# A gMLP and dilated-attention trunk on one core: combined weights made one stage earlier, the last two half-size products run tile by tile, saved key/value weights kept for every other unit

## The chip, the cores and the metric

The kernel runs on one core of a Trainium2 chip. A core has five engines with instruction queues of their own: TensorE (PE, matrix products; its weight loads are listed apart as PEld), VectorE (DVE), ScalarE (ACT), GpSimd (POOL) and SyncE (SP), which in this kernel issues the DMA transfers, one after the other in the order of its queue. The metric is the device time of the whole kernel in microseconds (us); lower is better. Matmul inputs are rounded to the format fp32r, so each fp32 matrix is kept as a pair hi + lo, and a product is made of three matmuls.

## The reference

Two layers over a sequence of 2048 tokens of width 1024, all fp32. The first is a gated MLP whose tokens are mixed within chunks of 128; the second is sliding-window attention in three dilation groups that read one shared K/V.

```python
def gmlp_layer(x, c, ada_w, ada_b, norm_g, w_in, sgu_g, w_s, b_s, w_out):
    shift, scale, gate = ada_mod(c, ada_w, ada_b, 3)
    h = rms_norm(x, norm_g) * (1 + scale) + shift
    u, v, z = jnp.split(h @ w_in, 3, axis=-1)              # each 2048 wide
    u = jax.nn.gelu(u)
    v = rms_norm(jax.nn.gelu(v), sgu_g)
    mixed = jnp.einsum('gts,bcsge->bctge', jnp.tril(w_s), v chunked) + b_s
    y = u * mixed * jax.nn.silu(z)
    return x + gate * (y @ w_out)                          # 2048 -> 1024

# shared_kv: k, v = split(norm(x) @ w_kv): 6 KV heads of 128, K normalised
# dilated_layer: q, z = norm(x) @ w_in: 24 query heads of 128 in 3 groups
#   (window, dilation) = (128, 1), (512, 4), (2048, 16); a banded softmax per head;
#   groups joined by the softmax of their log-sum-exp; x + gate * ((o * silu(z)) @ w_out)
```

## The kernel before

The sequence is cut into four quarters Q = 0..3 of 512 tokens. Each quarter passes through `layer_A` and then `proj_B`; each stage is a run of products over 512 tokens.

`layer_A` has four stages: v (`dense`, PSUM tiles pd_v), u and z (`dense_f`, pd_u and pd_z, eight blocks j each), and the output product y @ w_out (pd_o), called the out stage here. Quarter 0 makes the output product plainly (`dense`, tiles pd_o0). Quarters 1 to 3 make it with seven half-size products (`dense_s`, a Strassen-Winograd scheme, tiles pd_oQa and pd_oQb), each of eight steps k; a step is 2 token tiles x 3 matmuls on one weight unit. Four of the seven use combinations t1..t4 of the quadrants of w_out. `combine_out` makes these once: it loads the quadrants in 8 slabs, combines them with four POOL subtractions a slab (L349-L352) and stores the results to HBM, those of even k already split into hi and lo (arrays wqs), those of odd k unsplit (wq). The y operands are combined and split by `OutOperands` (`put`).

`proj_B` follows with three key/value blocks `kv_block` n = 2, 1, 0 and the query products between them, in the order kv 2, kv 1, q 2, kv 0, q 1, q 0, z. Blocks 2 and 1 are split in an early quarter and their eight split units are saved to HBM (arrays wk, 512 KB a unit); later quarters load these instead of splitting again (`kv_units`).

A weight unit is 128 x 512 of a weight. `raw_unit` loads it (256 KB, tiles raw_*), ACT writes hi (L246) and DVE, or POOL for some, writes lo (L250) into a tile w_* of a pool of eight buffers; `split_unit` loads a saved split unit (512 KB) and needs neither. All loads and stores stand in SP's single queue in program order as a scheduler settled it, and an issue that waits holds up those behind it.

**Fillers.** The attention of quarter Q-1 has no stage of its own. The generator `attend_local` is put on a list and `tick(part)`, called after every step of a product, advances it by `rate[0]` x part pieces. It runs during v, u and z of quarter Q; what is left is drained. A unit of attention is: transposes of Q and K on PE, scores ps (L1100-L1102), DVE bias and row maxima (L1105, L1108, L1109, L1112), ACT exponential (L1115), POOL on the diagonal block (L1123, L1124, L1126), transposes pp of the probabilities (L1143, L1157) and products po (L1176). POOL L1225 and DVE L1180 join the groups' outputs. `weave` advances `attend_local` and `combine_out` together, one piece of each per call: this is how `combine_out` runs during quarter 1.

Behind the out stage, `scale_out` stores the new residual (x1d, L818) and scales it (xr, L821); `transposed(1)` and `transposed(0)` turn its token tiles with PE transposes pt_b (L566), whose copies hkh and hkl (L572) are the left operand of pd_kv. `transposed(1)` (tiles 2 and 3) is called within the last of the seven products, `transposed(0)` (tiles 0 and 1) is handed on as `tail` and called within the first kv block.

## Time and profile before

| what | us |
|---|---|
| median of 3 runs (3076.18, 3084.06, 3090.19) | 3084.06 |
| the profiled execution's own time | 3080.11 |
| its span, first to last instruction | 3078.4 |
| PE busy | 2951.7 (96%) |
| DVE, ACT, POOL busy | 2100.3, 1658.5, 1014.2 |
| quarter 0: v 27.7-143.1, u to 252.9, z to 340.0, out to 429.0, kv/q/z to 659.7 | |
| quarter 1: v 659.7-766.9, u to 896.7, z to 1013.4, out to 1096.4, kv/q/z to 1341.3 | |
| quarter 2: v 1341.3-1453.0, u to 1576.0, z to 1693.7, out to 1776.2, kv/q/z to 2008.6 | |
| quarter 3: v 2008.6-2119.9, u to 2243.0, z to 2360.4, out to 2444.9, kv/q/z to 2795.5, end 3078.4 | |

Times within a profile count from the first instruction. A line of waits gives the engine that waits and for which tile and line, "<-" the instruction waited for, and then the total, the number and the longest of the waits. A line of windows gives, for each engine, the busy time and the number of instructions, in the order PE, PEld, DVE, ACT, POOL, and then the granted PE clock (1.00 is full), the mean busy share of the DMA engines and GB/s. A line of the timeline has the start, the duration and the instruction, and in brackets how long the engine idled ahead of it and for what.

### The profile page before, as it was taken

How to read it: one execution, taken by the hardware profiler on the slowest of the kernel's cores; microseconds unless marked ns; L12 is line 12 of the kernel's file. 1: busy time of each engine (PE TensorE's matmuls, PEld its weight loads, DVE VectorE, ACT ScalarE, POOL GpSimd, SP SyncE). 2: the span in 40 equal slices, each digit the busy share in tenths (PEclk: the TensorE clock that was granted, in tenths of full speed). 3: DMA queues.
4: the chain of work that ended last, by engine and by line, in shares of the span. 5: the costliest groups of instructions: out<-in, count | busy, mean ns of one | idle time of the engine just before them, and what ended most of it. 6: DMA issues, size and time to landing. Idle time of an engine off the chain costs nothing.

```text
span 3078.4 us, 45400 instructions
## 1 busy us (share of the span) xinstructions
PE 2951.7 (96%) x14784; PEld 2466.3 (80%) x14784; DVE 2100.3 (68%) x3576; ACT 1658.5 (54%) x3368; POOL 1014.2 (33%) x1232
## 2 busy tenths in 40 slices
PE   6999999999999999999999999999999999988999
PEld 5788878787788767788888878788887788867787
DVE  6788466774567777765677776856678677767762
ACT  4333345666456545566366455566466358857540
POOL 4147013344314323423134323423236031133332
PEclk9999999999999999999999999999999999999999
DMA  7899456677733687663433776743334776678742
GB/s 234 265 322 344 154 202 210 216 236 245 246 103 114 224 276 246 210 212 114 134 100 113 250 245 210 249 156 124 108 116 138 257 230 216 224 231 282 247 147 96
DMA packets 363073, 619.14 MB, mean 201 GB/s; under 512 B 38250, under 2 KB 137804, under 8 KB 362836
## 3 DMA queue, kind: packets, MB, share of 16 engines
q1 hardware_dynamic: 362836, 616.24, 61.1%
q8 instruction: 117, 1.92, 0.3%
q14 instruction: 120, 0.98, 0.1%
HBM read 489.61 MB, written 126.49 MB: 200 GB/s over the span
## 4 chain that ended last, share of the span: by engine, by line
PE 48%; DMA 7%; DVE 6%; issue 5%; POOL 3%; ACT 3%; SPq 1%; POOLq 0%; DVEq 0%; ACTq 0%
PE pd_v L293 5%; PE po L1176 3%; PE pd_kv L293 3%; PE pd_u L330 3%; PE pd_u L332 3%; PE pd_u L331 2%; PE pd_z L332 2%; PE pd_z L330 2%; PE pd_z L331 2%; DMA qt<-qd 2%; PE pm L756 1%; PE pf L1353 1%; PE pf L1354 1%; PE pf L1352 1%; PE pd_o2b L293 1%
## 5 line engine op out<-in xcount | busy, mean ns | idle before, releaser
L293 PE MATMUL pd_v<-w_v,hAh 128*128 128x512 f32 x1024 | 329.7, 403 | 3.5 <-ACT hAh L544 1.2
L293 PE MATMUL pd_kv<-w_kv,hkh 128*128 128x512 f32 x768 | 238.1, 392 | 9.2 <-DMA w_kv<-wk 3.8
L293 PEld LDWEIGHTS pd_v<-w_v,hAh 128*128 128x128 f32 x1024 | 190.1, 192 | 44.5 <-DVE w_v L250 2.8
L1115 ACT ACTIVATE pr<-pr,stat,rt 128x256 f32<-128x256 f32 (+1 forms) x320 | 177.6, 556 | 66.0 <-DVE stat L1109 40.1
L332 PE MATMUL pd_u<-hAh,w_u 128*128 128x512 f32 x512 | 202.5, 395 | 7.0 <-DVE w_u L250 7.0
L330 PE MATMUL pd_u<-hAh,w_u 128*128 128x512 f32 x512 | 208.3, 407 | 0.0
L330 PE MATMUL pd_z<-hAh,w_z 128*128 128x512 f32 x512 | 206.4, 403 | 0.0
L293 PE MATMUL pd_v<-w_v,hAl 128*128 128x512 f32 x512 | 203.3, 397 | 0.0
L332 PE MATMUL pd_z<-hAh,w_z 128*128 128x512 f32 x512 | 201.9, 394 | 0.0
L331 PE MATMUL pd_z<-hAl,w_z 128*128 128x512 f32 x512 | 201.1, 393 | 0.0
L331 PE MATMUL pd_u<-hAl,w_u 128*128 128x512 f32 x512 | 201.0, 393 | 0.0
L293 PEld LDWEIGHTS pd_kv<-w_kv,hkh 128*128 128x128 f32 x768 | 142.8, 188 | 43.0 <-ACT hkh L572 4.9
L1123 POOL TENSOR_TENSOR dg<-pr,ident 128x256 f32<-128x256 f32 x76 | 59.9, 788 | 343.8 <-ACT pr L1115 317.7
L246 ACT ACTIVATE w_u<-raw_u 128x512 fp32r<-128x512 f32 x128 | 78.4, 630 | 167.6 <-PE pd_u L332 89.0
L1176 PEld LDWEIGHTS po<-kv,pT 128*128 128x128 f32 x1200 | 147.8, 192 | 10.4 <-ACT pT L1026 3.7
L1176 PE MATMUL po<-kv,pT 128*128 128x128 f32 x1200 | 151.2, 276 | 2.0 <-ACT pT L1026 1.9
L246 ACT ACTIVATE w_z<-raw_z 128x512 fp32r<-128x512 f32 x128 | 78.0, 625 | 138.8 <-PE pd_z L332 58.6
L293 PE MATMUL pd_kv<-w_kv,hkl 128*128 128x512 f32 x384 | 148.5, 390 | 0.0
L250 DVE TENSOR_TENSOR w_u<-raw_u,w_u 128x512 fp32r<-128x512 f32 x128 | 101.2, 804 | 68.4 <-ACT w_u L246 66.8
L959 POOL TENSOR_SCALAR s_q<-s_q 128x4 f32<-128x4 f32 x96 | 23.3, 243 | 366.5 <-DVE s_q L958 338.6
L1105 DVE SCALAR_TENSOR_TENSOR pr<-dist,rt,ps 128x256 f32<-128x256 f32 (+1 forms) x320 | 122.5, 430 | 24.2 <-PE ps L1102 19.1
L250 DVE TENSOR_TENSOR w_z<-raw_z,w_z 128x512 fp32r<-128x512 f32 x128 | 117.6, 937 | 30.4 <-ACT w_z L246 27.9
(748 smaller groups left out, 8248.3 us busy)
## 6 DMA issues: line engine op xcount, KB each, us to landing
raw_q<-in_b_w_in_dram SPq DMA_DIRECT2D x144, 256.0 KB, 4.1
raw_v<-in_a_w_in_dram SPq DMA_DIRECT2D x128, 256.0 KB, 4.4
raw_u<-in_a_w_in_dram SPq DMA_DIRECT2D x128, 256.0 KB, 3.7
raw_z<-in_a_w_in_dram SPq DMA_DIRECT2D x128, 256.0 KB, 2.8
raw_o<-in_a_w_out_dram SPq DMA_DIRECT2D x104, 256.0 KB, 3.0
qt<-qd SPq DMA_DIRECT2D x96, 260.0 KB, 3.3
od<-ot SPq DMA_DIRECT2D x96, 256.0 KB, 2.9
w_kv<-wk SPq DMA_DIRECT2D x40, 512.0 KB, 5.1
```

Of the source, the lines that this page charges most:

```text
L246: nc.scalar.activation(hi, src, AF.Copy)
L250: e.tensor_tensor(lo, src, hi.bitcast(F32), ALU.subtract)
L293: last_mm[0] = nc.tensor.matmul(pt, a, u[:, w, :], start=f, stop=e, skip_group_check=more)
L330: nc.tensor.matmul(pts[i], wh, hh[:, k, :], start=k == 0, stop=False)
L331: nc.tensor.matmul(pts[i], wh, hl[:, k, :], start=False, stop=False)
L332: nc.tensor.matmul(pts[i], wl, hh[:, k, :], start=False, stop=k == KT - 1)
L756: nc.tensor.matmul(pm[:, t * P:(t + 1) * P], m[e // 8][:, t, (e % 8) * P:(e % 8 + 1) * P], wst[:, e // 2, :], start=True, stop=True)
L1105: nc.vector.scalar_tensor_tensor(pr[:, i, :], dist[:, 256 - w:256], u["rt"][:, h:h + 1], psc[:, i, :], ALU.mult, ALU.add)
L1115: nc.scalar.activation(pr[:, i, :], pr[:, i, :], AF.Exp, bias=mneg[:, i:i + 1], scale=u["rt"][:, h:h + 1], accum_out=lsum[:, i:i + 1])
L1123: nc.gpsimd.tensor_tensor(dg, prev, ident.unsqueeze(1).broadcast_to([P, hp, P]), ALU.mult)
L1176: nc.tensor.matmul(po[:, h * P:(h + 1) * P], u["pT"][h // hp][:, h % hp, j, :], u["kv"][:, j, kh, 1, :], start=j == 0, stop=j == nk - 1)
L1352: nc.tensor.matmul(pt, yb[:, 0, k, :], wh[:, k, :], start=k == 0, stop=False)
```

## The change

1. `combine_out` no longer runs beside the attention in quarter 1. It is put on the filler list at the start of quarter 0's out stage, with a rate of 1.6 where the rate was 0. It stages its slabs in tiles of the attention (qt, qT, pr, pT) instead of xin, as four loads of 256 KB a slab, and runs as a pipeline in which slab k is loaded while slab k-1 is stored. Only t2 and t3 at even k are stored split; t1 and t4, and odd k, are stored raw, and for raw units of t1 and t4 with k % 3 == 1 POOL makes the lo part.
2. The attention's rate goes from 1.4 to 1.5.
3. In quarters 1 to 3 the last two of the seven products run all 24 matmuls of token tile 0, then its additions and output, and then those of tile 1. `transposed(1)` comes after k = 2 of tile 1 of the last product.
4. Of the saved kv blocks only the even units are saved and loaded split; the odd ones are loaded raw and split each time.
5. `transposed(0)` is called at k = 6 of the first kv block instead of k = 4.
6. In `OutOperands`, half of the lo parts of operand "12" go from DVE to POOL.

```diff
 def kv_units(Q, n, nm):
-        if n == 0 or Q < 2 - n:
-            return wunits(w_kv, 0, n * 512, nm)
-        if Q > 2 - n:
-            return [split_unit(rows_of(wk2[n], k), f"{nm}{k}") for k in range(KT)]
-        us = wunits(w_kv, 0, n * 512, nm)
-        for k, u in enumerate(us):
-            nc.sync.dma_start(rows_of(wk2[n], k), u.bitcast(F32))
+        saved = n and Q > 2 - n
+        us = []
+        for k in range(KT):
+            if saved and k % 2 == 0:
+                us.append(split_unit(rows_of(wk2[n], k // 2), f"{nm}{k}"))
+                continue
+            us.append(raw_unit(w_kv[k * P:(k + 1) * P, n * 512:(n + 1) * 512], f"{nm}{k}"))
+            if n and Q == 2 - n and k % 2 == 0:
+                nc.sync.dma_start(rows_of(wk2[n], k // 2), us[k].bitcast(F32))
         return us
...
-                    if mid and pr == prs[0] and k == KT // 2:
+                    if mid and pr == prs[0] and k == KT - 2:
                         mid()
...
         def load(k):
-            hold[k] = [xp.tile([P, 2, 512], F32, tag="xin", name=f"co{k}{r}") for r in range(2)]
-            for r in range(2):
-                nc.sync.dma_start(hold[k][r], ...)
+            if k % 2:
+                t = [ap_.tile([P, 520], F32, tag="qt", name=f"co{k}{i}")[:, 0:512] for i in range(2)]
+                u = ap_.tile([P, 2, 512], F32R, tag="qT", bufs=1, name=f"co{k}")
+                t += [u[:, i, :].bitcast(F32) for i in range(2)]
+            else:
+                t = [ap_.tile([P, 512], F32, tag=tag, name=f"co{k}{tag}{i}") for tag in ("pr", "pT")
+                     for i in range(2)]
+            hold[k] = t
+            for i, d in enumerate(t):
+                r, c = divmod(i, 2)
+                nc.sync.dma_start(d, a_w_out[(8 * r + k) * P:(8 * r + k + 1) * P, c * 512:(c + 1) * 512])
...
         def store(k):
...
             for i, t in enumerate((t1, t2, t3, t4)):
-                if k % 2:
-                    nc.sync.dma_start(wq[i][rw, :], t)
+                if k % 2 or i not in wq2:
+                    nc.sync.dma_start(rows_of(wq[i], k), t)
                 else:
                     u = wp.tile([P, 2, 512], F32R, tag="w", name=f"wso{k}{i}")
                     nc.scalar.activation(u[:, 0, :], t, AF.Copy)
                     nc.gpsimd.tensor_tensor(u[:, 1, :], t, u[:, 0, :].bitcast(F32), ALU.subtract)
...
-        for k in range(KT):
-            load(k)
-            yield
-            yield
-            combine(k)
-            yield
-            store(k)
-            yield
+        for k in range(KT + 1):
+            if k < KT:
+                load(k)
+            yield
+            if k:
+                store(k - 1)
+            yield
+            if k < KT:
+                combine(k)
             yield
...
-        def product(pts, a, w, first, mid=None):
+        def product(pts, a, w, first, after=None, mid=None):
...
+            for tiles in ((0,), (1,)) if after else ((0, 1),):
+                for k in range(nk):
+                    if callable(ops) and k % 2 == 0:
+                        ops(None)
+                    for i in tiles:
+                        sl = slice(i * P, (i + 1) * P)
+                        mm3(pts[i], hh[:, k, sl], hl[:, k, sl], us[k], first and k == 0, k == nk - 1, True)
+                    tick(part * len(tiles) / 2)
+                    if mid and tiles == (1,) and k == 2:
+                        mid()
+                if after:
+                    after(tiles[0])
...
+        if mid:
+            product(y, "22", "t4", False, done21)
+            product(x, "s4", "22", False, done12, mid)
+            return
...
         if Q == 0:
-            rate[0] = 0
+            fillers.append(combine_out())
+            rate[0] = 1.6
...
-                self.put("12", j, r1, nc.vector)
+                self.put("12", j, r1, nc.gpsimd if j % 4 else nc.vector)
...
         if Q > 0:
-            main = attend_local(Q - 1, True)
-            fillers.append(weave(main, combine_out()) if Q == 1 else main)
-            rate[0] = 1.4
+            fillers.append(attend_local(Q - 1, True))
+            rate[0] = 1.5
```

How the change moves instructions is shown at two places. Rows give the line in the kernel they belong to, so lines of the changed kernel are some 25 higher from there on: its L1130, L1133, L1134, L1137, L1160, L1205 are L1105, L1108, L1109, L1112, L1135, L1180 of before, and its L843 is L818.

**DVE at the end of the attention in quarter 1.** pr_3_10 and pr_3_11 are the probabilities of the last unit, yos a half of the out stage's operand, w_o a unit of w_out, w_z one of the z stage. Before:

```order
L1105 SCALAR_TENSOR_TENSOR pr_3_11_8896<-dist,rt_3_1_8762,ps_3_11_8895 128x256
L861 TENSOR_TENSOR yos_8604<-st_ys_8859,yos_8604 128x512
L1108 TENSOR_REDUCE rt_3_1_8762<-pr_3_10_8877 128x2
L1105 SCALAR_TENSOR_TENSOR pr_3_11_8896<-dist,rt_3_1_8762,ps_3_11_8895 128x256
L1109 SCALAR_TENSOR_TENSOR stat_186<-rt_3_1_8762 128x2
L250 TENSOR_TENSOR w_o_3_9053<-raw_o_3_9054,w_o_3_9053 128x512
L1112 TENSOR_TENSOR stat_186<-stat_186,stat_187 128x2
L1108 TENSOR_REDUCE rt_3_1_8762<-pr_3_11_8896 128x2
L250 TENSOR_TENSOR w_o_4_9058<-raw_o_4_9059,w_o_4_9058 128x512
L1109 SCALAR_TENSOR_TENSOR stat_186<-rt_3_1_8762 128x2
L1112 TENSOR_TENSOR stat_186<-stat_186,stat_187 128x2
```

And in the changed kernel:

```order
L1130 SCALAR_TENSOR_TENSOR pr_3_11_8751<-dist,rt_3_1_8616,ps_3_11_8750 128x256
L1133 TENSOR_REDUCE rt_3_1_8616<-pr_3_10_8732 128x2
L1130 SCALAR_TENSOR_TENSOR pr_3_11_8751<-dist,rt_3_1_8616,ps_3_11_8750 128x256
L1134 SCALAR_TENSOR_TENSOR stat_184<-rt_3_1_8616 128x2
L250 TENSOR_TENSOR w_z_8964<-raw_z_8965,w_z_8964 128x512
L1137 TENSOR_TENSOR stat_184<-stat_184,stat_185 128x2
L1133 TENSOR_REDUCE rt_3_1_8616<-pr_3_11_8751 128x2
L1134 SCALAR_TENSOR_TENSOR stat_184<-rt_3_1_8616 128x2
L1137 TENSOR_TENSOR stat_184<-stat_184,stat_185 128x2
```

The unit now stands among the z stage's weight units, before the out stage's first ones: L861 and one of the two L250 are no longer between its rows.

**SP between the out stage and the kv blocks of quarter 2.** w_kv_0_k are the split units of kv block 2, raw_kv_0_k raw ones (the later numbers are block 1's), xr_t the residual's token tiles. Before:

```order
L263 DMA w_kv_0_0_16196<-wk_128 128x1024
L263 DMA w_kv_0_1_16198<-wk_128 128x1024
L818 DMA x1d<-xr_2_15412 128x1024
L818 DMA x1d<-xr_3_15414 128x1024
L263 DMA w_kv_0_2_16200<-wk_128 128x1024
L263 DMA w_kv_0_3_16202<-wk_128 128x1024
```

And in the changed kernel:

```order
L843 DMA x1d<-xr_2_15457 128x1024
L255 DMA raw_o_7_16124<-in_a_w_out_dram 128x512
L255 DMA raw_kv_0_1_16253<-in_w_kv_dram 128x512
L255 DMA raw_kv_0_3_16260<-in_w_kv_dram 128x512
L255 DMA raw_kv_0_5_16267<-in_w_kv_dram 128x512
L255 DMA raw_kv_0_7_16274<-in_w_kv_dram 128x512
L255 DMA raw_kv_0_1_16463<-in_w_kv_dram 128x512
L843 DMA x1d<-xr_3_15459 128x1024
L255 DMA raw_kv_0_3_16470<-in_w_kv_dram 128x512
L263 DMA w_kv_0_0_16250<-wk_126 128x1024
L843 DMA x1d<-xr_0_15453 128x1024
L263 DMA w_kv_0_2_16257<-wk_126 128x1024
```

The raw loads of both blocks now come ahead, the first split unit w_kv_0_0 stands behind the stores of xr_2 and xr_3, and w_kv_0_2 behind that of xr_0, which is ready only when the last product's tile 0 has been added up.

More of the change, by code (lines that the diff above doesn't have):

```diff
@@ L66, in trunk @@
     wt = [[dp.tile([512, 512], F32, name=f"wt{b}_{i}") for i in range(4)] for b in range(4)]
-    wq = [dp.tile([512, 512], F32, name=f"wq{i}") for i in range(4)]
-    wq2 = [dp.tile([512, 2, 512], F32, name=f"wqs{i}") for i in range(4)]
-    wk2 = {n: dp.tile([D, 2, 512], F32, name=f"wk{n}") for n in (1, 2)}
+    wq = [dp.tile([D, 512], F32, name=f"wq{i}") for i in range(4)]
+    wq2 = {i: dp.tile([512, 2, 512], F32, name=f"wqs{i}") for i in (1, 2)}
+    wk2 = {n: dp.tile([512, 2, 512], F32, name=f"wk{n}") for n in (1, 2)}
     fillers = []
@@ L257, in raw_unit @@
             tc.keep_in_program_order(ld)
-        split(u[:, 0, :], u[:, 1, :], raw, ordered)
+        split(u[:, 0, :], u[:, 1, :], raw, ordered or pool)
         return u
@@ L354, in store @@
         def store(k):
[L355 to L356 removed]
+            t1, t3, t4, t2 = hold.pop(k)
             for i, t in enumerate((t1, t2, t3, t4)):
[L358 to L359 removed]
+                if k % 2 or i not in wq2:
+                    nc.sync.dma_start(rows_of(wq[i], k), t)
                 else:
```

46 lines of the change are left out of this document (20 added, 26 removed).

## The prediction

> **What bounds the kernel now.** I read the page's busy shares first, then the waits of PE stage by stage, the window rows for the granted clock in the same stretches, the timeline around the costliest wait, and last the list of DMA issues.
>
> ```profile
> PE 2951.7 (96%) x14784; PEld 2466.3 (80%) x14784; DVE 2100.3 (68%) x3576; ACT 1658.5 (54%) x3368; POOL 1014.2 (33%) x1232
> ```
>
> PE is the bound, and the change takes no product away. What can be won is what PE loses: waits, and stretches at half clock behind waits. The places that the edits touch are therefore priced one by one.
>
> The first sign of where to look is one stretch, v to z with the attention beside it, in two quarters:
>
> ```profile
> 659.70:1013.40 353.70, 339.97 (x1743) 285.55 (x1742) 207.84 (x379) 211.37 (x409) 122.72 (x120) 0.98 0.53 176
> 1341.30:1693.60 352.30, 347.79 (x1873) 297.36 (x1872) 228.03 (x448) 206.18 (x391) 117.24 (x154) 0.99 0.38 119
> ```
>
> Quarter 1 has 130 PE instructions fewer than quarter 2 and yet takes 1.4 us longer. PE idles 353.7 − 340.0 = 13.7 us in quarter 1 and 4.5 us in quarter 2, and its clock is a hundredth lower, 3.5 us. Quarter 1 is where `combine_out` runs: it loses about 9.2 + 3.5 = 12.7 us more.
>
> **Part 1: combining leaves quarter 1 (edit 1).** The waits there (660 to 860 us) and the windows around the two clock drops:
>
> ```profile
> PE pd_u L332 <- DVE w_u L250: 4.6, 2, 2.4
> PE pp L1157 <- ACT pr L1115: 2.4, 2, 2.2
> PE pd_v L293 <- DVE w_v L250: 1.2, 1, 1.2
> ...
> 767.00:785.00 18.00, 13.36 (x50) 10.48 (x49) 11.49 (x20) 9.78 (x23) 9.36 (x10) 0.81 0.83 284
> 820.00:828.00 8.00, 7.53 (x33) 6.39 (x34) 4.50 (x7) 5.29 (x12) 0.00 (x0) 0.79 0.89 269
> ```
>
> Waits are 4.6 + 2.4 + 1.2 = 8.2 us, lost clock (1 − 0.81) × 18 = 3.4 and (1 − 0.79) × 8 = 1.7: 13.3 us, which agrees with the 12.7. The DMA share of 0.83 and 0.89, against 0.38 over quarter 2, and POOL's 9.36 us in 18 tie it to the combining: its loads and stores stand in SP's queue ahead of weight loads, and its split copies hold buffers of the pool w. I take −12, with 0 and −13.3 as bounds (0 if the 1.5 rate only makes attention press harder there).
>
> These stretches also bear on the clock. Waits of at most 2.4 us, one behind the other, were enough for a drop to half clock. The Trainium skill ("TensorE: Matmul & The Clock Gate", Part 1: The HAM clock gate) says that the clock falls after at least one idle window of about 3.4 us; no single wait here is that long, so by the page the 5.1 us of clock would not be this cause's, and part 1 would be worth 8.2. The rows at 767 and 820 us speak against that reading, and the measurement decides.
>
> **Part 2: the end of the attention (rate 1.5, no weave).** In quarters 1, 2 and 3 the last unit ends at the z stage's end with the same wait (860 to 1020, 1680 to 1692, 2350 to 2362 us); the first two of the three like lines, and the clock behind each:
>
> ```profile
> PE pp L1143 <- POOL pr L1126: 4.0, 2, 3.4
> ...
> PE pp L1143 <- POOL pr L1126: 4.0, 2, 3.4
> ...
> 1010.40:1016.40 6.00, 6.00 (x15) 4.76 (x16) 4.90 (x8) 2.75 (x5) 2.80 (x3) 0.50 0.05 17
> 1690.60:1695.60 5.00, 4.99 (x13) 4.03 (x14) 3.86 (x7) 2.29 (x5) 1.76 (x3) 0.50 0.02 7
> 2357.60:2361.20 3.60, 3.60 (x10) 2.92 (x11) 2.78 (x5) 1.12 (x3) 1.46 (x2) 0.53 0.01 5
> ```
>
> Waits 3 × 4.0 = 12.0; clock 0.50 × 6.0 + 0.50 × 5.0 + 0.47 × 3.6 = 7.2; together 19.2 us. The chain that is late runs from the scores over DVE and ACT to POOL; DVE and POOL in it:
>
> ```profile
> 998.91 1.11 DVE L861 TENSOR_TENSOR yos<-st_ys,yos 128x512 fp32r<-128x512 f32 x1 [0.89 <-ACT yos L860]
> 1001.00 0.68 DVE L250 TENSOR_TENSOR w_o<-raw_o,w_o 128x512 fp32r<-128x512 f32 x1
> 1002.26 0.68 DVE L250 TENSOR_TENSOR w_o<-raw_o,w_o 128x512 fp32r<-128x512 f32 x1
> 1007.67 1.48 POOL L1225 TENSOR_TENSOR st_o<-st_o,stat 128x512 f32<-128x512 f32 x1
> ```
>
> With 1.5 instead of 1.4 the unit ends some z blocks earlier. Its pieces stay as far apart on PE as before, since both kernels put as many matmuls between ps and pp; what changes is who stands in the chain. L861 (1.11, with 0.89 of idle ahead of it: the operands of the out stage) is gone from it, one of two L250 (0.68) too, and POOL's L1225 (1.48) comes earlier: 4.16 us against the 4.0 waited. The cover is thin, so I leave a little: −16, bounds 0 and −19.2. The upper bound for harm is +4, one more wait of that size.
>
> **Part 3: kv 1 to q 2 in quarter 1 (edit 4's stores).**
>
> ```profile
> PE pd_q12b L293 <- DVE w_q L250: 3.7, 2, 3.4
> PE pd_q12a L293 <- ACT hs_k L931: 1.2, 1, 1.2
> ...
> 1159.00:1164.00 5.00, 4.47 (x13) 3.51 (x14) 4.68 (x8) 1.45 (x3) 0.00 (x0) 0.66 0.53 174
> ...
> wk<-w_kv SPq DMA_DIRECT2D x16, 512.0 KB, 5.7
> ```
>
> Eight stores of 512 KB stand on SP ahead of the first q weights, each waiting for its split; sixteen in two quarters become eight. If the q loads come first, the waits 3.7 + 1.2 and the clock (1 − 0.66) × 5 = 1.7, in all 6.6, go. I take −5, bounds 0 and −6.6. Block 2's stores in quarter 0 halve at no gain: no wait of theirs is to be seen there.
>
> **Part 4: out stage to kv (edits 3, 4, 5, 6).** The waits of the three quarters, in order:
>
> ```profile
> PE pt_b L566 <- DVE xr L821: 2.5, 3, 1.4
> PE pd_kv L293 <- DVE w_kv L250: 2.0, 2, 1.2
> PE pd_kv L293 <- ACT hkh L572: 0.8, 1, 0.8
> ...
> PE pt_b L566 <- DVE xr L821: 2.9, 3, 1.5
> PE pd_kv L293 <- DMA w_kv<-wk: 1.7, 1, 1.7
> PE pd_kv L293 <- ACT hkh L572: 0.8, 1, 0.8
> ...
> PE pt_b L566 <- DVE xr L821: 3.8, 3, 1.8
> PE pd_kv L293 <- DMA w_kv<-wk: 2.1, 1, 2.1
> PE pd_o3b L293 <- DMA w_o3t<-wqs: 1.6, 2, 1.0
> PE pd_kv L293 <- ACT hkh L572: 0.8, 1, 0.8
> ```
>
> That is 5.3 + 5.4 + 8.3 = 19.0 us. Token tile 0's additions, residual and scaling (DVE, with the store x1d) now run under tile 1's 24 matmuls, so pt_b of tile 0 has its operand while PE still works; `transposed(0)` two steps later helps the same wait. Per quarter this covers pt_b and hkh, 3.3 to 4.6 us. Against it: the eight units of a product must now all lie in the pool until tile 1 has read them, so no buffer comes free while tile 0 runs, and the loads bunch behind it; the first split unit stands on SP behind two stores, the third behind one that waits for tile 0's end.
>
> ```profile
> x1d<-xr SPq DMA_DIRECT2D x16, 512.0 KB, 2.7
> w_kv<-wk SPq DMA_DIRECT2D x40, 512.0 KB, 5.1
> raw_kv<-in_w_kv_dram SPq DMA_DIRECT2D x56, 256.0 KB, 3.0
> ```
>
> A raw unit lands 2.1 us sooner than a split one, and then needs ACT and DVE, which after the last product are busy with the residual. Following these rows by hand, one wait of 1.5 to 2 us stays at tile 1's end and one of about 1.3 for a late split; 3 × 3.3 = 10 of the 19.0 remain. I take −9. Bounds: −19, and for harm +9, if each quarter is 3 us worse from the late units. Eight more splits on DVE in these quarters cost DVE time only; PE waits where they come late, which is in this bound. Edit 6 moves lo parts to POOL (33% busy): nothing.
>
> **Part 5: combining enters quarter 0's out stage (edit 1, the other end).**
>
> ```profile
> 340.00:429.00 89.00, 89.00 (x402) 73.67 (x401) 39.67 (x65) 27.39 (x53) 2.40 (x4) 1.00 0.38 126
> 200.00:225.00 25.00, 25.00 (x128) 21.31 (x127) 16.44 (x16) 7.30 (x12) 17.61 (x13) 1.00 1.04 348
> ...
> L349 POOL TENSOR_TENSOR co<-co 128x512 f32<-128x512 f32 x8 | 10.3, 1288 | 37.3 <-DMA co<-in_a_w_out_dram 37.3
> L363 POOL TENSOR_TENSOR wso<-co,wso 128x512 fp32r<-128x512 f32 x16 | 22.0, 1390 | 41.7 <-ACT wso L362 41.6
> ```
>
> That stage has PE always busy, DMA at 0.38, POOL almost idle. It receives 32 combinations × 1.29 = 41 us of POOL, 8 splits × 1.39 = 11 us, and loads and stores that a stretch with DMA at 1.04 carried without a PE wait. All fits in 89 us; the rest runs on into kv. The stage's own loads pass the new ones on SP, each of which waits for a staging tile, so a little is lost: +3, bounds 0 and +13.3 (the whole stall of part 1 moves along). Later, in each out stage of quarters 1 to 3, the eight units of t1 and t4 at even k must be split again, 8 × 0.68 (DVE, as at 1001.00) to 8 × 1.39 (POOL) = 5 to 11 us under 82 us of matmuls; I count nothing, since the o stage shows only the one wait w_o3t of 1.6 on its weights.
>
> One rule speaks against this. A subtraction on DVE slows beside POOL's combining:
>
> ```profile
> 695.31 5.08 DVE L250 TENSOR_TENSOR w_v<-raw_v,w_v 128x512 fp32r<-128x512 f32 x3 [3.88 <-ACT w_v L246]
> 696.53 1.62 POOL L351 TENSOR_TENSOR co<-co,co 128x512 f32<-128x512 f32 x1
> ```
>
> These take 1.69 us each, against 0.68 at 1001.00. The Trainium skill ("SBUF — State Buffer", Who interferes with whom) has it that a DVE instruction with two SBUF inputs and a GpSimd one lock a shared port pair against each other; the trace agrees with its 1.69. By it, DVE and POOL would follow one another, 39.7 + 52 = 92 us in a stage of 89, and part 5 would be at its upper bound.
>
> **Sum.** −12 − 16 − 5 − 9 + 3 = −39. Against the profiled execution's 3080.1 this gives 3041.1; the median of the runs lies 4.0 above that execution, so the forecast is **3045 us**. With parts 1 to 5 near their bounds together (−58 or −17) its own range is 3026 to 3067.
>
> **Rivals.**
> A. The waits between out and kv come back in another form: part 4 is +9 instead of −9, so 3063. For it: the w pool is full through tile 0, and split units stand behind stores. Against it: pt_b's cause is plainly gone. Chance 0.20.
> B. The end-of-attention wait stays (part 2 is 0): 3061. The same chain, ps to POOL, is as long, and other work of DVE fills the gaps; against it, 4.16 us leave it. 0.08. That this part of the change does nothing is this rival.
> C. Combining stalls quarter 0 as it stalled quarter 1 (part 5 +13.3): 3055. For it, the 1.69 above; against it, PE's full busy share beside DMA at 1.04. 0.10.
> D, slower: four split kv units a quarter come late, because each stands behind a store or raw load on SP that waits for the residual. Each costs the landing that a store ahead does not cover, 5.1 − 2.7 = 2.4 us, and a clock drop like that at 820 us, 1.7: 4 × 4.1 = 16.4 a quarter, 49 in three. Taken with the other parts, without part 4, that is 3084 − 30 + 49 = 3103. It decides once w_kv_0_0 is issued after the last product's tile 0 has ended. Against it: only three of the stores come between, and two of them are ready in the product before. 0.08.
>
> The forecast keeps 0.54.
>
> **How the numbers follow.** A measurement of this kernel can tell about 0.5% from no change, 3068.6 to 3099.5. Faster than that: the forecast but for 0.03, six tenths of A, three quarters of B and C, 0.51 + 0.12 + 0.135, about 0.77. Slower: D, 0.08. Same: the rest, 0.15. The range goes from 3028 to 3076: below, parts at their bounds together are not likely; above, it takes in A, B and C with 9 to 13 us of their own spread.
>
> **What would show it.** Part 1: no wait of pd_u for w_u over 1 us in quarter 1, and window rows at clock 1.00 there. Part 2: the L1143 line (now some 25 lines lower) under 1 us and no half clock at the z stage's end. Part 3: no pd_q12b wait. Part 4: pt_b for xr under 1 us a quarter, a wait of 1 to 2 us for w_kv left. Part 5: the out stage of quarter 0 at 89 to 92 us, with DVE's L250 there slower than 0.68. Wrong it would be with new clock drops in kv (A, D), or a quarter 0 over 95 us (C).

## The result, and the profile after

The changed kernel takes 3066.81 us (median of 7 runs, 3056.51 to 3071.75) against 3084.06 us before (7 runs, 3076.18 to 3090.19): the ratio is 0.9941, 95% interval 0.9923 to 0.9959. It is faster, as forecast, but by 17 us where the forecast said 39; 3066.8 lies within the stated range of 3028 to 3076. Its profiled execution spans 3063.5 us.

Of the page, the busy shares have hardly moved:

```profile
PE 2944.6 (96%) x14784; PEld 2462.6 (80%) x14784; DVE 2103.2 (69%) x3596; ACT 1669.3 (54%) x3400; POOL 1041.4 (34%) x1248
```

The windows of the changed kernel answer to those of before: quarter 0's out stage, and v to z of quarters 1, 2 and 3.

```profile
338.54:447.16 108.62, 94.05 (x401) 75.61 (x400) 53.97 (x63) 31.38 (x61) 50.47 (x39) 0.95 0.74 252
...
678.20:1013.70 335.50, 332.57 (x1760) 282.47 (x1759) 189.06 (x380) 196.78 (x391) 62.79 (x74) 1.00 0.40 125
1332.90:1686.10 353.20, 348.30 (x1890) 298.17 (x1889) 229.05 (x448) 205.79 (x392) 116.40 (x154) 1.00 0.38 120
1997.30:2352.30 355.00, 350.55 (x1889) 300.28 (x1888) 226.94 (x448) 205.11 (x390) 117.20 (x154) 0.99 0.38 120
```

Quarter 1 went from 353.7 to 335.4 us, with PE idle for 2.9 us instead of 13.7: the forecast gain is there. Quarter 0's out stage went from 89.0 to 108.6 us, with PE idle for 14.6: that is more than the whole gain of quarter 1. In quarters 2 and 3, v to z did not become shorter. The same by stages, in the profiled executions; a stage is counted from its first matmul to the first of the next, and the time between the ends of the last stages (3073.3 and 3058.0) is split:

| stretch | before | after | difference |
|---|---|---|---|
| quarter 0: v to z, with the start | 340.0 | 338.5 | -1.5 |
| quarter 0: out stage | 89.0 | 108.6 | +19.6 |
| quarter 0: the rest | 230.7 | 231.1 | +0.3 |
| quarter 1: v to z | 353.7 | 335.4 | -18.3 |
| quarter 1: out stage, kv 2 and kv 1 | 134.6 | 137.5 | +2.9 |
| quarter 1: q 2 | 47.7 | 40.8 | -7.0 |
| quarter 1: the rest | 145.5 | 141.0 | -4.5 |
| quarter 2: v to z | 352.4 | 353.2 | +0.8 |
| quarter 2: out stage, kv 2 and kv 1 | 132.9 | 128.4 | -4.5 |
| quarter 3: v to z | 351.8 | 355.0 | +3.2 |
| quarter 3: out stage, kv 2 and kv 1 | 135.7 | 130.1 | -5.6 |
| quarters 2 and 3: the rest | 759.2 | 758.4 | -0.8 |

What PE waits for in quarter 0's out stage of the changed kernel (total, times, longest):

```profile
PE pd_o L296 <- ACT w_o L246: 8.6, 2, 4.8
PE pt_b L590 <- DVE xr L846: 3.7, 1, 3.7
PE pd_o L296 <- DVE w_o L250: 2.3, 2, 1.9
```

One step back, what ACT waits for, what SP's queue waits for, and ACT's and SP's timelines at the first stall (PE stands still from 385 to 390 us):

```profile
ACT w_o L246 <- DMA wqs<-wso: 31.5, 5, 11.6
...
SPq L373 <- POOL wso L372: 10.9, 7, 3.1
SPq L355 <- DMA wq<-co: 8.2, 6, 3.0
...
389.09 1.67 ACT L246 ACTIVATE w_o<-raw_o 128x512 fp32r<-128x512 f32 x3 [11.56 <-DMA wqs<-wso]
...
376.57 6.27 SPq L355 DMA_DIRECT2D co<-in_a_w_out_dram  x4
386.12 0.33 SPq L373 DMA_DIRECT2D wqs<-wso  x1
...
390.45 1.21 SPq L255 DMA_DIRECT2D raw_o<-in_a_w_out_dram  x2
```

ACT could not make the next w_o because the buffer it needed held wso, a split copy of a combination, whose store left SP only at 386.12; and w_o's own loads stood in the same queue until 390.45. Two causes lie in these lines, and the experiments had to tell them apart.

At the end of the attention, the waits in quarters 1, 2 and 3 are:

```profile
PE po L1201 <- POOL pT L1175: 1.6, 1, 1.6
PE pp L1168 <- POOL pr L1151: 0.9, 1, 0.9
...
PE po L1201 <- POOL pT L1175: 2.6, 2, 1.5
PE pp L1168 <- POOL pr L1151: 0.3, 1, 0.3
...
PE po L1201 <- POOL pT L1175: 3.6, 2, 2.1
PE pp L1168 <- POOL pr L1151: 0.6, 1, 0.6
```

The wait of 4.0 us for pp (L1143 before) is almost gone, and a wait of po, one link further down the same chain, has come in its place. From the out stage to kv 1, quarter 1 shows a new wait for a kv weight:

```profile
PE pd_kv L296 <- DVE w_kv L250: 3.4, 1, 3.4
...
PE pt_b L590 <- DVE xr L846: 1.3, 1, 1.3
```

### The profile page after: what moved, and what is told of

It is laid out like the page before. It is cut to its first block, busy times and chain, and to the rows that moved or that the text cites. A ratio compares the mean times of both kernels' runs of the same rounds, so it can differ in the third digit from the quotient of the medians.

```text
span 3063.5 us, 45564 instructions
## 1 busy us (share of the span) xinstructions
PE 2944.6 (96%) x14784; PEld 2462.6 (80%) x14784; DVE 2103.2 (69%) x3596; ACT 1669.3 (54%) x3400; POOL 1041.4 (34%) x1248
## 4 chain that ended last, share of the span: by engine, by line
PE 63%; DVE 11%; DMA 9%; issue 8%; POOL 5%; ACT 3%; SPq 1%; POOLq 0%; DVEq 0%; ACTq 0%
PE pd_v L296 8%; PE pd_kv L296 6%; PE pd_u L333 4%; PE pd_u L335 4%; PE pd_u L334 4%; PE po L1201 3%; PE pd_z L333 3%; PE pd_z L334 3%; PE pd_z L335 3%; PE pm L780 2%; DMA qt<-qd 2%; PE pq L1089 1%; PE pd_o2b L296 1%; DMA x1d<-xr 1%; PE pf L1377 1%
## 5 line engine op out<-in xcount | busy, mean ns | idle before, releaser
L1130 DVE SCALAR_TENSOR_TENSOR pr<-dist,rt,ps 128x256 f32<-128x256 f32 (+1 forms) x320 | 122.8, 430 | 38.4 <-PE ps L1127 24.2
L250 DVE TENSOR_TENSOR w_o<-raw_o,w_o 128x512 fp32r<-128x512 f32 x104 | 99.5, 980 | 71.8 <-ACT w_o L246 59.9
L250 DVE TENSOR_TENSOR w_u<-raw_u,w_u 128x512 fp32r<-128x512 f32 x128 | 99.5, 791 | 50.4 <-ACT w_u L246 50.3
```

The costliest lines, as they stand in the source:

```text
L250: e.tensor_tensor(lo, src, hi.bitcast(F32), ALU.subtract)
L1130: nc.vector.scalar_tensor_tensor(pr[:, i, :], dist[:, 256 - w:256], u["rt"][:, h:h + 1], psc[:, i, :], ALU.mult, ALU.add)
```

## The experiments

All kernels start from the changed one; ratios are to runs of the kernel before on the same chip. Stage times are from one profiled execution each; in the stretches that an edit did not touch, such times differ between kernels by up to 9 us in the longest (quarter 3 behind its kv 1: 570 to 579) and by some 4 us in v to z of quarter 2, so small differences are only read where a wait names them. The runs were made on several chips, on which the kernel before took from 3079.7 to 3084.6 us, so kernels are compared by their ratios and intervals before their medians.

| kernel | median, us | ratio to before, 95% interval | quarter 0's out stage |
|---|---|---|---|
| before | 3084.06 | | 89.0 |
| the changed kernel | 3066.81 | 0.9941 (0.9923 to 0.9959) | 108.6 |
| combining's transfers issued by POOL | 3140.79 | 1.0194 (1.0173 to 1.0216) | 112.9 |
| combining at rate 0.8 | 3062.80 | 0.9938 (0.9919 to 0.9958) | 101.3 |
| POOL's arithmetic alone | 3112.58 | 1.0104 (1.0082 to 1.0126) | 95.6 |
| attention at rate 1.4 | 3057.33 | 0.9926 (0.9901 to 0.9950) | 107.7 |
| split copies in a tile of their own | 3062.38 | 0.9928 (0.9909 to 0.9947) | 105.0 |
| exponential earlier | 3066.07 | 0.9948 (0.9929 to 0.9967) | 108.2 |
| without tile sequence | 3067.50 | 0.9948 (0.9934 to 0.9963) | 108.7 |
| all kv units saved | 3080.67 | 0.9995 (0.9983 to 1.0007) | 108.2 |
| combining back in quarter 1 | 3052.57 | 0.9906 (0.9889 to 0.9922) | 89.0 |
| own tile, POOL issues | 3143.49 | 1.0197 (1.0179 to 1.0215) | 189.9 |
| own tile, POOL issues stores, rate 1.4 | 3100.77 | 1.0061 (1.0046 to 1.0076) | 151.8 |
| no split copies | 3050.04 | 0.9887 (0.9864 to 0.9911) | 89.4 |
| combining back, rate 1.4 | 3059.06 | 0.9913 (0.9884 to 0.9943) | 89.0 |
| combining back, rate 1.4, no split copies | 3067.09 | 0.9948 (0.9932 to 0.9965) | 88.9 |
| no split copies, rate 1.4 | 3043.01 | 0.9880 (0.9862 to 0.9897) | 89.2 |

### What stalls quarter 0's out stage

**Combining's transfers issued by POOL.**

```diff
-                nc.sync.dma_start(...)      # all loads and stores of combine_out
+                nc.gpsimd.dma_start(...)
```

> The changed kernel with one difference: the loads and stores of combine_out are issued by POOL, not by SP; POOL's arithmetic, the bytes and the staging tiles stay. In the changed kernel quarter 0's out stage takes 108.6 us (89.0 before) and PE waits there 8.6 + 2.3 us for w_o and 3.7 for xr. Theory S (SP's queue: weight loads stand behind combining's loads and stores that wait for a tile or for POOL): the stage is at 89 to 94 us, whole kernel about 3050. Theory P (POOL's subtractions slow DVE and the splits): POOL works as much, the stage stays at 105 or more and the kernel at 3067. Theory D (the DMA engines are full): the same bytes move in the same stage, 105 or more, 3067.

Measured: 3140.8 us and a stage of 112.9. Theory S, that SP's order alone is the cause, did not come true: ACT's w_o still sat 23.0 us behind the stores wqs<-wso. The run does not acquit SP either, since the scheduler now moved combining to the kernel's very beginning, where the first quarter's v stage went from 115 to 167 us.

**Combining at half the rate.**

```diff
-            rate[0] = 1.6
+            rate[0] = 0.8
```

> The changed kernel with combine_out advanced at rate 0.8 instead of 1.6 in quarter 0's out stage; the second half of it runs on beside the kv blocks. Theory S: with twice the distance between a slab's steps its transfers are ready when SP reaches them, the stage is at 91 to 96 us and the kv blocks lose at most 4, whole kernel 3050 to 3056. Theories P and D: loss goes with the work, half of it (about 10 us) stays in the stage at 99 us and the other half turns up in the kv blocks; whole kernel about 3065.

Measured: 3062.8 us, the stage at 101.3 and quarter 0's rest at 243.2 instead of 231.1. Against before, the loss spread out and stayed: 12.3 + 12.5 = 25 us in the two, against 20 in the changed kernel; the whole kernel was no slower (ratio 0.9938 against 0.9941). That is what theories P and D expected, but the traces also show SP still standing behind combining's steps (no weight load was issued from 370 to 392 us), so the rate does not set how far apart the steps stand in SP's queue.

**POOL's arithmetic alone**, the real combining moved to q 1, q 0 and z.

```diff
         if Q == 0:
-            fillers.append(combine_out())
+            fillers.append(pool_only())     # 40 subtractions, no transfers
...
+                    fillers.append(combine_out())   # behind make_hA, rate 2.0
```

> The changed kernel with combine_out moved on to the last three products of quarter 0's second half (q 1, q 0, z), and in its old place, the out stage, a stand-in that does POOL's arithmetic alone: the 32 combinations and 8 more subtractions of 128x512 on tiles that are set once, at the same rate and with no transfers; its results are not used. Theory S: without transfers nothing holds SP, the out stage is at 89 to 91 us. Theory P: DVE's splits are as slow as before the move and the stage stays at 100 or more. Theory D: 89 to 91. What q 1 to z lose by the real combining shows in their own stages (122 us before); if it is under 5, the whole kernel is about 3051.

The stage was 95.6 us and decides nothing: the scheduler moved the stand-in, which depends on nothing, to the kernel's start, and the real loads into the out stage. The stand-in's first subtraction runs on POOL at 13.1 us. The start and the first v stage became 40 us longer (PE waited 26.0 us for POOL's hAl), and q 0 and z, beside the real combining's end, 18 us.

**The split copies in a tile of their own.**

```diff
-                    u = wp.tile([P, 2, 512], F32R, tag="w", name=f"wso{k}{i}")
+                    u = ap_.tile([P, 2, 2, 2, P], F32R, tag="kT", bufs=1, name=f"wso{k}{i}")
```

> The changed kernel with one difference: the two split copies wso of every even slab lie in the attention's tile kT (free in quarter 0) and no longer in the pool w, which the weight units use. POOL's and ACT's work, the transfers and SP's queue stay. In the changed kernel's out stage (108.6 us) ACT's hi copies of w_o sit behind the stores wqs<-wso for 31.5 us in 5 stretches, because two of the eight buffers of w are held. Theory W (held buffers): these waits go, the stage is at 89 to 95 us, whole kernel 3047 to 3054. Theory S (SP blocked by combining's stores and loads): SP still waits some 45 us in them, the stage stays at 103 or more, whole kernel 3062 or more.

The stage fell only to 105.0 us. Its window, and what ACT and SP wait for:

```profile
337.31:442.27 104.96, 96.13 (x401) 76.75 (x400) 52.24 (x65) 29.84 (x60) 49.77 (x39) 0.95 0.80 273
...
ACT wso L372 <- DMA wqs<-wso: 14.2, 4, 4.8
...
SPq L374 <- POOL wso L373: 21.5, 6, 5.5
```

w_o no longer waits for a held buffer, as theory W said; but the copies wso now hold ACT itself (w_o's copies stand behind them in its queue), and SP waits for wso twice as long. The edit has a price of its own: the tile kT has one buffer (`bufs=1`), so the second copy of a slab waits for the store of the first, the 14.2 us above, which the changed kernel does not have. So the run shows that the copies still stall the stage when they do not lie in the pool w, but not how much of the 19.6 us the held buffers were. By its times alone theory S came true here; the run without split copies, below, decides between them.

**Own tile, and POOL issues the transfers**, from slab 2 on so that nothing starts early; and a candidate in which POOL issues the stores alone, with rate 1.4.

```diff
-                nc.sync.dma_start(d, a_w_out...)
+                (nc.sync if k < 2 else nc.gpsimd).dma_start(d, a_w_out...)
-                nc.sync.dma_start(rows_of(wq[i], k), t)
+                nc.gpsimd.dma_start(rows_of(wq[i], k), t)      # wqs likewise
```

> The changed kernel with both blockers of quarter 0's out stage taken away: the split copies in a tile of their own, and all stores of combining and its loads from slab 2 on issued by POOL (the first two slabs' loads stay on SP, so that nothing starts early). With the copies alone out of the pool w the stage went from 108.6 to 105.0 us, and SP still waited for wso, wq and co. Theory S (what is left is SP's order): the stage is at 89 to 95 us, whole kernel 3045 to 3053. Theory P (DVE's splits slowed by POOL, or the DMA engines): POOL's arithmetic and all bytes are still there, the stage stays at 101 or more and PE waits for w_o on DVE.

> A candidate for a better kernel: the changed kernel with the attention's rate at 1.4 (which alone gave 3057.3 against 3066.8), the split copies in their own tile, and combining's stores issued by POOL with its loads left on SP. Theory S: the out stage of quarter 0 falls to 90 to 97 us, and with the 9 us of the rate the whole kernel is at 3040 to 3048. Theory P: the stage is at 101 or more, whole kernel 3053 to 3056.

Both became worse than anything expected, 189.9 and 151.8 us for the stage. The first one's window, what PE and ACT wait for, and POOL between two slabs:

```profile
339.62:529.56 189.94, 106.25 (x402) 82.66 (x400) 56.97 (x65) 29.07 (x60) 79.00 (x95) 0.76 0.42 145
...
PE pd_o L296 <- ACT w_o L246: 81.5, 6, 19.1
...
ACT wso L372 <- DMA wqs<-wso: 53.4, 4, 16.2
...
365.20 0.56 POOL L368 DMA_DIRECT2D wq<-co  x1 [2.68 <-issue]
367.81 0.55 POOL L368 DMA_DIRECT2D wq<-co  x1 [2.04 <-issue]
```

A transfer issued by POOL costs it 0.55 us and some 2 us of standing still ahead of it, so a slab takes longer, and ACT stands behind wso all the while. The stage got longer although SP was free of combining's stores, and PE waited for ACT's w_o (81.5 us) and hardly for DVE's (2.2), where theory P expected it: what hurts is w_o behind wso, whatever delays wso.

**No split copies.**

```diff
-    wq2 = {i: dp.tile([512, 2, 512], F32, name=f"wqs{i}") for i in (1, 2)}
+    wq2 = {}                     # every combination is stored unsplit
```

> The changed kernel with all combinations stored unsplit: no split copies wso at all, so eight copies on ACT and eight subtractions on POOL fewer in quarter 0; the out stages of quarters 1 to 3 split all their units themselves. Loads, combinations and stores of combining stay on SP. Theory A (the split copies are what stalls quarter 0: they take buffers of w, and ACT's copies of w_o stand behind them in ACT's queue): quarter 0's out stage at 89 to 95 us, out stages of quarters 1 to 3 at most 1 us longer each, whole kernel 3047 to 3054. Theory S (SP's order: the raw stores wait for POOL and the loads for the stores, with w_o's loads behind): the stage at 101 or more, whole kernel 3058 or more.

This settles it: 89.4 us, 3050.0 for the kernel. Its window, what SP still waits for, and the subtractions of w_o on DVE in the same stage of three kernels (before, changed, this one: count, busy time, mean ns of one):

```profile
338.54:427.89 89.35, 89.05 (x402) 73.66 (x400) 49.99 (x65) 27.28 (x53) 40.32 (x31) 1.00 0.83 285
...
SPq L355 <- DMA wq<-co: 11.5, 8, 3.7
...
L250 DVE TENSOR_TENSOR w_o<-raw_o,w_o 128x512 fp32r<-128x512 f32 x25 | 17.3, 692 | 29.8 <-ACT w_o L246 29.7
L250 DVE TENSOR_TENSOR w_o<-raw_o,w_o 128x512 fp32r<-128x512 f32 x25 | 27.4, 1128 | 45.1 <-ACT w_o L246 33.6 <-DMA co4pT<-in_a_w_out_dram 11.5
L250 DVE TENSOR_TENSOR w_o<-raw_o,w_o 128x512 fp32r<-128x512 f32 x25 | 23.1, 944 | 28.3 <-ACT w_o L246 28.2
```

POOL works 40.3 us in the stage, the DMA share is 0.83, above the changed kernel's 0.74, SP still waits for combining's stores, DVE's subtractions are slower by 0.25 us each, and PE loses nothing. Theories P, D and S fall; the eight split copies are the cause, in the places where they hold what w_o needs. The edit also takes eight of POOL's subtractions away (50.5 to 40.3 us of it in the stage), but the 40 us that stay cost nothing. The copies also had a use: without them the out stages of quarters 1 to 3 take 86.5, 85.5 and 85.7 us instead of 83.6, 82.3 and 83.0, 8.8 us together where at most 1 us each was expected. PE waits there 4.1, 4.2 and 4.2 us for POOL's lo part of a raw unit (L250).

### What the move was worth

**Combining back beside quarter 1's attention.**

```diff
-            fillers.append(combine_out())      # quarter 0's out stage: rate 0 again
+            fillers.append(weave(main, combine_out()) if Q == 1 else main)
```

> The changed kernel with combining put back beside the attention of quarter 1, woven and staged in xin as before (the new storage format, the rate of 1.5 and all other edits stay). The prediction's part 1 with the measured part 5: quarter 0's out stage goes back to 89 us (-19.6), v to z of quarter 1 go from 335 to between 349 and 353 (+14 to +18), so the move alone was worth within 6 us, whole kernel 3061 to 3066. Rival: without the rate's change and the old store format the stall in quarter 1 is much smaller (v to z under 343), the move itself was a loss and the whole kernel is at 3055 or less.

3052.6 us: the rival's side. Quarter 0's out stage is at 89.0 and v to z of quarter 1 at 345.7, only 10.3 us above the changed kernel.

```profile
659.03:1004.76 345.73, 338.97 (x1760) 285.84 (x1759) 200.88 (x379) 206.18 (x401) 113.11 (x112) 0.99 0.53 174
```

PE idles 6.8 us there, not 13.7 as before the change. The stall in quarter 1 was already about halved without the move, by the new storage format and the rate (the run with rate 1.4 below, 348.6 us, puts some 5 us to the format); the move to quarter 0 with its split copies then cost 19.6 to win 10.3. In the changed kernel the move as such was a loss: 11 us by the ratios (0.9941 against 0.9906, whose intervals do not overlap), 14 by the medians.

### The attention's rate

**Rate 1.4, with combining in quarter 0.**

```diff
-            rate[0] = 1.5
+            rate[0] = 1.4
```

> The changed kernel with the attention's rate at 1.4 as before, and no weave. Theory T (the higher rate only trades the wait of pp for POOL L1151 at the z stage's end for a wait of po for the POOL part of pT, one link later): v to z of quarters 2 and 3 stay within 2 us of 353.2 and 355.0, with the pp wait of 4.0 and the half clock back, whole kernel 3067 within noise. Rival R (the rate won its 5 us a quarter and something else lost them): v to z of quarters 2 and 3 are each 4 us or more longer, whole kernel 3077.

**Rate 1.4, with combining back in quarter 1**, and the same without split copies.

> Combining back beside the attention of quarter 1 (3052.6 with rate 1.5), now with the attention's rate at 1.4; all other edits stay. Theory T2 (the rate of 1.5 costs some 9 us in this kernel, as it did with combining in quarter 0: 3066.8 against 3057.3): whole kernel 3042 to 3046, mostly by the z and out stages of quarters 2 and 3. Rival (that difference was the chance position of the steps, not the rate): 3050 to 3056.

> Combining beside the attention of quarter 1 with rate 1.4 and all combinations stored unsplit. Theory A (the split copies carry the stall there too): v to z of quarter 1 fall from 346 to 337 to 341 us, whole kernel 5 us under that with split copies. Theory S: v to z stay within 2 us of it.

With combining in quarter 0, v to z of quarters 2 and 3 at 1.4 are 352.4 and 353.5 us, within the 2 us of theory T, but the wait for pp does not come back, and the median is lower than either theory had it (3057.3 against 3066.8, and 3043.0 against 3050.0 without split copies). The intervals of the ratios overlap, so that 1.4 is faster is not shown by the times. In the traces the gain lies in the out stages of quarters 1 to 3, 81.5, 80.3 and 81.0 us against 83.6, 82.3 and 83.0, where PE's waits for split units of w_out (w_o1t to w_o3t) are 0, 0.3 and 1.2 us against 1.9, 2.6 and 2.2. With combining back in quarter 1, 1.4 is no faster (3059.1 against 3052.6, 0.9913 against 0.9906): theory T2 falls, and the time lies above the rival's range too. The end of the attention in quarter 3, first with combining in quarter 0 and then with it back, both at 1.4:

```profile
PE po L1201 <- POOL pT L1175: 2.0, 2, 1.1
...
PE pp L1167 <- POOL pr L1150: 4.0, 2, 3.4
```

The same rate gives the wait of 4.0 in one and 2.0 at the next link in the other: what decides is where the steps fall, since the fraction that the rate's counter carries depends on all fillers ahead. The wait of 4.0 was thus never the rate's own. Without split copies, the old place in quarter 1 has v to z at 344.0 us instead of 348.6, not at the 337 to 341 that theory A expected, and the out stages pay more than that: 88.0, 85.1 and 86.1 against 82.6, 83.2 and 83.0; that kernel is the slower one (3067.1 against 3059.1 us). So in the old place the split copies were only a part of the stall.

**The exponential that joins two groups comes earlier.** This moves it and its subtraction from the third to the second step of a unit.

```diff
-            nc.vector.tensor_tensor(e1, stat[0][:, b, k4], e1, ALU.subtract)   # in att_3
-            nc.scalar.activation(e1, e1, AF.Exp)
+            ... the same two lines at the end of att_2
```

> The changed kernel with one small thing moved: the exponential that joins groups 0 and 1 (L1160 and L1161) comes right behind the unit's other exponentials, so that ACT does not load its exponential table again behind the Silu of the z stage. Theory L (the new wait of po for pT comes from ACT's table loads of 1.28 us, behind which DVE stands at L1196): the waits of po for POOL L1175 at the end of z (1.6, 2.6, 3.6 us in quarters 1 to 3) fall under 1 each, v to z of these quarters lose 1 to 5 us each, whole kernel about 3059. Rival (POOL's own order, L1250 between the two L1175, sets it): waits stay, 3067.

No gain: 3066.1 us, and theory L falls. In quarter 3, pp waits 1.9 us and po 3.4. DVE and POOL there, between pp and the last pT:

```profile
2329.04 1.78 DVE L250 TENSOR_TENSOR w_o<-raw_o,w_o 128x512 fp32r<-128x512 f32 x1
2331.08 1.43 DVE L886 TENSOR_TENSOR yos<-st_ys,yos 128x512 fp32r<-128x512 f32 x1
2332.43 0.41 DVE L1175 TENSOR_TENSOR pT<-pp,pT 128x256 f32<-128x256 f32 x1
...
2331.92 1.49 POOL L1251 TENSOR_TENSOR st_o<-st_o,stat 128x512 f32<-128x512 f32 x1
2333.37 1.85 POOL L1176 TENSOR_TENSOR pT<-pT,dg 128x256 f32<-128x256 f32 x2
```

The rival, POOL's own order, holds only in part: POOL's scaling L1251 kept pT back for 0.5 us, from the end of DVE's L1175 at 2332.84. More of the wait is DVE's order, in which a weight unit and a half of the out stage's operand, 3.2 us together, stand between pp and that pT.

### The kv units and the tile sequence

**All kv units saved, as before.**

```diff
-            if saved and k % 2 == 0:
+            if saved:                   # and all eight stored
```

> The changed kernel without edit 4: all eight units of kv blocks 2 and 1 are saved and loaded split, as before. The prediction's parts 3 and 4: q 2 of quarter 1 goes back from 40.8 to about 47 us with its w_q wait of 3.7, and in quarters 2 and 3 a wait of about 2 us for w_kv from HBM comes back; quarter 1's new w_kv wait of 3.4 us with its half clock goes. Sum +6 - 5 + 4, whole kernel about 3072. Rival: the wait in quarter 1 only changes its place and the loads were hidden anyway, within 2 us in all, 3067.

3080.7 us, 14 more than the changed kernel and no faster than before (0.9995, 0.9983 to 1.0007). The waits that come back, in quarters 1, 2 and 3:

```profile
PE pd_q12b L294 <- DVE w_q L250: 4.2, 2, 2.3
...
PE pd_kv L294 <- DMA w_kv<-wk: 3.5, 2, 2.9
...
PE pd_kv L294 <- DMA w_kv<-wk: 3.7, 2, 3.5
```

q 2 of quarter 1 is at 46.8 us instead of 40.8, and the kv blocks of quarters 2 and 3 at 49.8 and 51.4 instead of 46.1 and 47.1. This edit carries most of what the change won.

**Without the tile sequence.**

```diff
-            product(y, "22", "t4", False, done21)
-            product(x, "s4", "22", False, done12, mid)
+            product(y, "22", "t4", False); done21(0); done21(1)
+            product(x, "s4", "22", False, None, mid); done12(0); done12(1)   # mid at k = 5
```

> The changed kernel without edit 3: the last two products of quarters 1 to 3 run both tiles step by step as before. In the changed kernel out stage and first kv blocks take 137.5, 128.4 and 130.1 us. The prediction's part 4: the waits for pt_b and hkh come back, 3.3 to 4.6 us a quarter, so 141, 132 and 134 and the whole kernel at 3079. Rival N (sequencing wins at pt_b what it loses at weight units that come free late): each within 1.5 us of the changed kernel, whole kernel 3067.

```profile
PE pt_b L594 <- DVE xr L850: 2.5, 3, 1.1
...
PE pt_b L594 <- DVE xr L850: 2.7, 3, 1.3
...
PE pt_b L594 <- DVE xr L850: 2.3, 3, 0.9
```

The waits for xr come back in every quarter (1.3, 0.2 and 1.3 with the sequence), and out stage to kv 1 take 139.2, 131.2 and 130.5 us instead of 137.5, 128.4 and 130.1: 5 us in the traces. The medians differ by 0.7 us, less than they can tell. It helps, by less than forecast.

### A kernel that beats both

**No split copies, rate 1.4.**

> A candidate for a better kernel: the changed kernel without split copies in combining (alone 3050.0) and with the attention's rate at 1.4 (alone 3057.3, against 3066.8 with 1.5). If the two add up, 3040 to 3044; if the rate's 9 us were the chance position of its steps (with combining in quarter 1, 1.5 was the faster by 6.5), 3047 to 3054. Quarter 0's out stage is expected at 89 to 91 us and out stages of quarters 1 to 3 at 84 to 87.

3043.0 us (5 runs, 3038.9 to 3045.0), ratio 0.9880 (0.9862 to 0.9897): 19 us faster than the changed kernel by the ratios, 24 by the medians. Most of it is the split copies, 17 us alone by either. What the rate adds is not shown: by the ratio it is 2 us on top of 0.9887, whose interval overlaps almost wholly, though the median fell in the range in which the two were expected to add up.

## Why the prediction was right or wrong

The direction was right, the size was not: 17 us of 39. By its parts, in the profiled executions; 1.8 us of each of the quarters 1 to 3 only changed stages (16 more PE instructions in v to z, 1873 and 1890 in quarter 2's rows: the last unit's po, which before ran in the out stage) and are put back here. In quarter 1, part 2 is its waits and its half clock (4.0 + 3.0 us before, by the prediction's figures, 2.5 + 0 after), part 1 what is left of v to z, and the kv blocks are counted under part 3.

| part | forecast | measured |
|---|---|---|
| 1. combining leaves quarter 1 | -12 | -15.6 |
| 2. end of the attention | -16 | -4.5, -1.0 and +1.4 in quarters 1 to 3: -4.1 |
| 3. kv 1 to q 2 in quarter 1 | -5 | -7.0 in q 2, +2.2 in kv: -4.8 |
| 4. out stage to kv | -9 | -8.4 in the kv blocks, +4.4 in the out stages: -4.0 |
| 5. combining enters quarter 0 | +3 | +19.6 |
| stretches that no part names | 0 | -6.5 |

The three parts that were to carry the gain, 1, 2 and 5, came to -25 in the forecast and to -0.1 in the traces. What is left of the gain is parts 3 and 4, and 6.5 us that no part names, so it is in good part luck that the time fell as forecast and lies in the range. The range's own upper end was not the sum of its bounds either: 0 + 4 + 0 + 9 + 13.3 is +26, where the prediction has -17.

**Part 5 is the step that failed most.** Its words were "All fits in 89 us", from busy times: POOL almost idle, DMA at 0.38 beside a stretch at 1.04. That judgement was right and was not the question. The run without split copies has POOL at 40 us and DMA at 0.83 in that stage, and loses nothing. What was not priced is what combining holds while it waits: two of eight weight buffers from ACT's copy until the store has landed, over POOL's and SP's queues, and ACT's order behind it. Part 1 had named the held buffers as a cause in quarter 1, and the same cause should have been carried over to the new place. The upper bound of 13.3 was taken from the old place too; a stall has no fixed size that moves with the work, and here it was 19.6. Rival C, which named this side, had the right sign and the wrong mechanism: DVE's subtractions do slow beside POOL, 692 to 944 ns, but that is not what PE waited for. The same holds for the rule of the Trainium skill ("SBUF — State Buffer", Who interferes with whom) that was weighed there, that a DVE instruction with two SBUF inputs and a GpSimd one contend: the trace agrees in that DVE slowed, and the run at 89.4 us shows that by itself it cost PE nothing.

**Part 2.** The step that failed is "DVE and POOL in it": the 4.16 us of intruders went out of the chain to pp, and its wait fell from 4.0 to 0.9, 0.3 and 0.6, as said; but the chain was followed only as far as pp. Two of the intruders only moved on by one link: the operand yos (L861, now L886), which was to be "gone", and the scaling L1225 (now L1250), which was to come "earlier", stand between pp and po, where z has only 12 matmuls. DVE and POOL in quarter 3 of the changed kernel:

```profile
2329.10 0.68 DVE L886 TENSOR_TENSOR yos<-st_ys,yos 128x512 fp32r<-128x512 f32 x1
...
2330.26 0.72 POOL L1175 TENSOR_TENSOR pT<-pT,dg 128x256 f32<-128x256 f32 x1 [1.43 <-DVE pT L1174]
2330.94 1.49 POOL L1250 TENSOR_TENSOR st_o<-st_o,stat 128x512 f32<-128x512 f32 x1
2332.39 1.16 POOL L1175 TENSOR_TENSOR pT<-pT,dg 128x256 f32<-128x256 f32 x1
```

The half clock behind the wait went in quarters 1 and 2; in quarter 3 it is 0.50 over 6.8 us (2332.6 to 2339.4), 3.4 us lost instead of 1.7. Rival B was the nearer one, one link on. The runs at rate 1.4 add that the position, which the rate sets only together with all other fillers, decides which of the two waits appears.

**Part 1** was right in sign and 3.6 us small in the trace, beyond its bound of -13.3 (its list of waits left out one of 0.9, of pd_v for ACT's w_v); the run with combining back shows that part of it came from the storage format and the rate, since the place itself was then worth 10.3. Of the two causes it named, the split copies that hold buffers were some 4.5 us in that place, with the eight that the new format leaves (348.6 to 344.0 without them, at rate 1.4).

**Part 3** won its wait in q 2, and lost part of it again in a step that was passed over, in kv 1, where PE waits 3.4 us for w_kv. The order of DVE is what the rows show:

```profile
1132.30 1.15 ACT L246 ACTIVATE w_kv<-raw_kv 128x512 fp32r<-128x512 f32 x2
...
1131.91 1.11 DVE L614 TENSOR_TENSOR hob<-st_b,hob 128x512 fp32r<-128x512 f32 x1 [3.11 <-ACT hob L611]
...
1137.49 1.28 DVE L250 TENSOR_TENSOR w_kv<-raw_kv,w_kv 128x512 fp32r<-128x512 f32 x2
```

ACT's hi copies of the last two units were done at 1133.5. DVE came to their lo parts only at 1137.5, behind operands of the query products (hob) and sums (acc_gb). Block 1 is split here in both kernels; which edit moved DVE's order no run separates. Together part 3 is -4.8, as forecast.

**Part 4.** The kv blocks of quarters 2 and 3 gained 8.4 us, close to the forecast. With all units saved 8.0 of them are lost again, without the tile sequence 3.0, so the alternating units carry most of it. The term that failed is "I count nothing", which the prediction has in its part 5 for the out stages of quarters 1 to 3: these lost 4.4 us. PE waits there for split units (quarters 1, 2 and 3 of the changed kernel, where before only quarter 3 had such a wait, of 1.6):

```profile
PE pd_o1b L296 <- DMA w_o1t<-wqs: 1.9, 3, 0.9
...
PE pd_o2a L296 <- DMA w_o2t<-wqs: 2.6, 4, 1.3
...
PE pd_o3b L296 <- DMA w_o3t<-wqs: 2.2, 4, 0.7
```

So it is not the raw units themselves that come late. The loads of the split ones stand in SP's queue between raw loads that wait for DVE's splits (in quarter 2 the load at 1717.1 follows 7.3 us of five raw loads). That the raw units cause this is argued, not shown: at rate 1.4 the same units are raw and the waits are 0, 0.3 and 1.2 us. Rival A did not come: the waits for xr are 1.3, 0.2 and 1.3 us. Rival D neither: w_kv waits 0.5 and 0.2 us in quarters 2 and 3.

**The clock.** The half-clock stretches of quarter 1's u stage are gone with their waits of 2.4 us, which fits the reading that was chosen over that of the Trainium skill ("TensorE: Matmul & The Clock Gate", Part 1: The HAM clock gate), by which the clock falls after at least one idle window of about 3.4 us. The two waits for w_o in quarter 0, 8.6 us, brought drops of their own: 0.95 over the 108.6 us of the stage, some 5 us of the 19.6.

## What to carry to other kernels

When work is moved into a stage, ask first what it holds while it waits (buffers of a shared pool, a place in an in-order queue) and for how long, and only then whether the engines have time for it: here the engines had time, and eight small copies that used the weight pool and ACT's queue cost 20 us. A stall's size belongs to its place and is not carried along as a bound: 13.3 us in the old place, 19.6 in the new. Follow a late chain to its last link, since a wait taken away at one link comes back at the next where the work that stood in it has only moved on by one.
